# Row scales kept on chip for the gates, and the low parts of k stored on all 128 partitions for the score products

## The chip, the cores and the metric

The kernel runs on one core of a Trainium2 chip. The metric is the device time of one execution in microseconds (us). Before the change it is 1217.34 us, the median of three runs that lay between 1215.89 and 1218.22 us.

The engines are named as in the profile: PE is TensorE's matmul, PEld its weight load, DVE is VectorE, ACT is ScalarE, POOL is GpSimd and SP is SyncE, which here issues most DMAs. Each engine works through its own queue in order, and waits on semaphores.

## The reference: what is computed

One transformer-like block over a sequence of S = 1024 rows and D = 1024 columns in fp32. The parts that matter here:

```python
proj = rms_norm(x, norm1_g) @ w_in            # 1024 -> 3*512 (q, k, v) + 512 (xl) + 512 (gl)
q, k = rms_norm(q, q_norm_g), rms_norm(k, k_norm_g)      # per head, 8 heads of 64
...
for blk in range(S // 128):                    # stick-breaking attention, causal
    z = einsum('bqhd,bkhd->bhqk', q[:, q0:end], k[:, :end]) / sqrt(64)
    log_one_minus = where(mask, log_sigmoid(-z), 0)
    suffix = cumsum(log_one_minus, axis=3, reverse=True) - log_one_minus
    w = where(mask, exp(log_sigmoid(z) + suffix), 0)
    out = w @ v
...
lru = rg_lru(causal_conv(xl)) * gelu(gl)       # a gated linear recurrence
x = x + concat([attn, lru]) @ w_out
x = x + square(relu(rms_norm(x, norm2_g) @ w_up)) @ w_down
```

## The kernel before

**Precision.** A matmul operand is split into a high part (rounded to fp32r) and a low part (the remainder, also fp32r). A full product is three matmuls, low by high, high by low and high by high (`mm3`, lines 70 to 73).

**Stages.** First x is loaded, transposed and split (`hTh`, `hTl`). The norm's row scale `rstd1` is not multiplied into x; it is applied after the projection. Then come the q, k, v projection of head pair 0, the xl projection with the linear recurrence (`lru_tile`), and from about 137 us to 452 us of the span a mixed stage: attention of all four head pairs, the projections of pairs 1 to 3, and the gates. The list `ORDER` (line 27) fixes the sequence in which the program traces these pieces: `Aphc` is attention of pair p, head h, rows 256c to 256c+255, `Ipt` the projection of pair p for rows 256t and on, `Gcs` gate tile c for half s, `O` and `W` load weights, `Y` sums MLP weights by DMA. From the traced program a planner at build time, with its own simulated timeline (`schedule_with_timeline_sim=True`), lays down the order of each engine's queue, so that pieces interleave. The mixed stage is followed by the output projection (about 452 to 560 us) and the MLP (to the end).

**Projection of a head pair** (`in_proj`, lines 193 to 238; it runs 16 times, 4 pairs by 4 blocks of 256 rows). Two groups of 24 matmuls give 128 rows each of q, k and v. ACT scales the rows out of PSUM into `raw`; DVE normalizes them. Then q is laid out as `qs` so that for head 0 its 64 columns of high part come first and its 64 columns of low part second, and for head 1 the other way round; k's high part is written twice side by side (`ks`, line 222), and k's low part once (`kl`, line 223, a POOL subtraction of 128x128 for each 128 rows). PE transposes these by multiplying with the identity (lines 228, 233 and 237), and the results are copied to `qT` (ACT, line 229), `kH` (DVE, line 234, 128x512) and `kL` (DVE, line 238, 128x256). So `qT[:, h]` holds high and low part of head h on two halves of the 128 partitions, `kH[:, h]` holds the high part of k on both halves, and `kL` holds head 0's low part on partitions 0 to 63 and head 1's on 64 to 127.

**Scores** (`attention`, lines 431 to 434). For 128 query rows and up to 512 key rows a score product is two matmuls that add into one PSUM bank z: `qT[:, h]` by `kH[:, h]` over all 128 partitions, which gives (high + low of q) by high of k, and `qT[hs, h]` by `kL[hs]` over the 64 partitions of this head, which gives high of q by low of k. On the diagonal a third, bf16 matmul adds the mask (line 434). There are 96 such products. Then ACT computes two sigmoids (lines 436, 437), DVE a reversed product scan (line 441), POOL a multiplication (line 442), PE transposes the weights (line 452), ACT and DVE split them (lines 456, 457) and PE multiplies with v (line 461).

**Row scales.** `scale_row` (line 259) writes `rstd1` to DRAM as `rs_d`, from where it is read as one row broadcast to 128 partitions. In the recurrence part the tile `rsb` (128x1024) is loaded that way (line 355); it lives in the pool `lru`, which is closed before the attention. In `gate` (line 479, eight times) a 128x512 tile `y` is loaded from `rs_d` again (line 483, issued by SP); SP must first wait until the buffer, which shares the tag `raw` with `in_proj`, is free. Then DVE multiplies the projection in PSUM by it (line 487, out `gx`).

Of the kernel before, what the change touches and what calls it, by code (L numbers as in the profile page):

```python
# [9 lines left out]
F32 = mybir.dt.float32  # L10
# [9 lines left out]
P = 128  # L20
# [23 lines left out]
def kernel(ctx, tc, x, norm1_g, w_in, conv_w, conv_b, w_rg, b_rg, w_ig, b_ig,  # L44
# [106 lines left out]
    hTh = hp.tile([P, KC, S], F32R, name="hTh")  # L151
    hTl = hp.tile([P, KC, S], F32R, name="hTl")
    qkvE = pool(left1, "qkvE")
    wp = pool(left1, "wp", bufs=8)
    mp = pool(left1, "misc")

# [31 lines left out]

    def in_proj_open(p, qp):
        return (qp.tile([P, 2, S], F32R, tag="qT", name=f"qT{p}"), qp.tile([P, 2, S], F32R, tag="kH", name=f"kH{p}"),  # L190
                qp.tile([P, S], F32R, tag="kL", name=f"kL{p}"), qp.tile([P, NT, 2, P], F32R, tag="vv", name=f"vv{p}"))

    def in_proj(p, qkv, ws, tp):
        qT, kH, kL, vv = qkv
        raw = mp.tile([P, 2, 4, HD], F32, tag="raw", name=f"raw{p}{tp}", bufs=2)
        for tt in range(2):
            t = 2 * tp + tt
            pd = bank(ps_d, [384], f"pd{p}{t}")
            for kc in range(KC):
                wh, wl = ws[kc]  # L200
                mm3(pd, hTh[:, kc, t * P:(t + 1) * P], hTl[:, kc, t * P:(t + 1) * P], wh, wl, kc == 0, kc == KC - 1)
            rs = rstd1[:, t:t + 1]
            nc.scalar.mul(raw[:, tt].rearrange("p a d -> p (a d)"), pd[:, 0:256], rs)
            pvv = pd[:, 256:384].rearrange("p (h d) -> p h d", h=2)
            nc.scalar.mul(vv[:, t, :, 0:HD], pvv, rs)
            nc.vector.scalar_tensor_tensor(vv[:, t, :, HD:P], pvv, rs, vv[:, t, :, 0:HD].bitcast(F32), op0=ALU.mult, op1=ALU.subtract)  # L206
        sq = mp.tile([P, 8, HD], F32, tag="sq", name=f"sq{p}{tp}")
        raw8 = raw.rearrange("p t a d -> p (t a) d")
        nc.vector.tensor_tensor(sq, raw8, raw8, op=ALU.mult)
        ssq = small.tile([P, 8], F32, tag="ssq8", name=f"ssq{p}{tp}")  # L210
        nc.vector.tensor_reduce(ssq, sq, axis=AX.X, op=ALU.add)
        rstd = rsqrt_mean(ssq, HD, 8)
        nc.vector.tensor_tensor(raw8, raw8, rstd.unsqueeze(2).broadcast_to([P, 8, HD]), op=ALU.mult)
        nc.gpsimd.tensor_tensor(raw[:, :, 0:2, :], raw[:, :, 0:2, :], qkg, op=ALU.mult)
        qs = mp.tile([P, 2, 2, 2, HD], F32R, tag="qs", name=f"qs{p}{tp}")
        ks = mp.tile([P, 4, 2, HD], F32R, tag="ks", name=f"ks{p}{tp}")
        kl = mp.tile([P, 2, 2, HD], F32R, tag="kl", name=f"kl{p}{tp}")
        for h in range(2):
            nc.scalar.copy(qs[:, :, h, h, :], raw[:, :, h, :])
            lo_part(nc.vector, qs[:, :, h, 1 - h, :], raw[:, :, h, :], qs[:, :, h, h, :])  # L220
        for tt in range(2):
            nc.scalar.copy(ks[:, 2 * tt:2 * tt + 2], raw[:, tt, 2:4, :].unsqueeze(2).broadcast_to([P, 2, 2, HD]))
            lo_part(nc.gpsimd, kl[:, tt], raw[:, tt, 2:4, :], ks[:, 2 * tt:2 * tt + 2, 0, :])
        cols = slice(256 * tp, 256 * tp + 256)
        pq = bank(ps_t, [2, 256], f"pq{p}{tp}")
        for h in range(2):
            for tt in range(2):
                nc.tensor.matmul(pq[:, h, tt * P:(tt + 1) * P], qs[:, tt, h].rearrange("p a d -> p (a d)"), identr, start=True, stop=True)
        nc.scalar.copy(qT[:, :, cols], pq)
        pk = bank(ps_t, [2, 256], f"pk{p}{tp}")  # L230
        for h in range(2):
            for tt in range(2):
                nc.tensor.matmul(pk[:, h, tt * P:(tt + 1) * P], ks[:, 2 * tt + h].rearrange("p a d -> p (a d)"), identr, start=True, stop=True)
        nc.vector.tensor_copy(kH[:, :, cols], pk)
        pl = bank(ps_t, [256], f"pl{p}{tp}")
        for tt in range(2):
            nc.tensor.matmul(pl[:, tt * P:(tt + 1) * P], kl[:, tt].rearrange("p a d -> p (a d)"), identr, start=True, stop=True)
        nc.vector.tensor_copy(kL[:, cols], pl)


    right1 = ExitStack()
# [108 lines left out]

    lstack = ExitStack()
    lp = pool(lstack, "lru", bufs=2, side="right")
    rsb = lp.tile([P, S], F32, name="rsb", bufs=1)
    for ch in range(2):
        nc.sync.dma_start(rsb[:, 512 * ch:512 * ch + 512], rs_row[:, 512 * ch:512 * ch + 512].broadcast_to([P, 512]))
    bd = {}
# [57 lines left out]
    def attention(p, h, c, qkv):  # L414
        qT, kH, kL, vv = qkv
        hs = slice(HD * h, HD * h + HD)
        os = slice(HD - HD * h, P - HD * h)
        wrow = []
        for r in (2 * c, 2 * c + 1):
            n = (r + 1) * P  # L420
            wps = {}
            nxt = None
            qr = slice(r * P, (r + 1) * P)
            for k0 in range((n - 1) // 512 * 512, -1, -512):
                kn = min(n - k0, 512)
                diag = k0 + kn == n
                g = ap.tile([P, 516], F32, tag="g", name=f"g{p}{h}{r}{k0}", bufs=NG)
                w = ap.tile([P, 512], F32, tag="w", name=f"w{p}{h}{r}{k0}", bufs=NW)
                wps[k0 // 512] = w
                z = bank(ps_z, [512], f"z{p}{h}{r}{k0}")[:, :kn]  # L430
                nc.tensor.matmul(z, qT[:, h, qr], kH[:, h, k0:k0 + kn], start=True, stop=False)
                nc.tensor.matmul(z, qT[hs, h, qr], kL[hs, k0:k0 + kn], start=False, stop=not diag)  # L432
                if diag:
                    nc.tensor.matmul(z[:, kn - P:kn], identb, maskb, start=False, stop=True)  # L434
                    nc.gpsimd.memset(g[:, kn:kn + 1], 1.0)
                nc.scalar.activation(g[:, :kn], z, AF.Sigmoid, scale=-1.0)  # L436
                nc.scalar.activation(w[:, :kn], z, AF.Sigmoid)
                if not diag:
                    nc.vector.tensor_copy(g[:, kn:kn + 1], nxt)
                gr = g[:, :kn][:, ::-1]  # L440
                nc.vector.tensor_tensor_scan(gr, gr, gr, g[:, kn:kn + 1], op0=ALU.mult, op1=ALU.bypass)  # L441
                mark(nc.gpsimd.tensor_tensor(w[:, :kn], w[:, :kn], g[:, 1:kn + 1], op=ALU.mult))  # L442
                nxt = g[:, 0:1]
            wrow.append(wps)
        av = bank(ps_a, [256], f"av{p}{h}{c}")
        for m in range(c + 1):
            pw = bank(ps_w, [512], f"pw{p}{h}{c}{m}")

            blocks = [(0, 0), (0, 1), (1, 0), (1, 1)] if m < c else [(0, 0), (0, 1), (1, 1)]
            for i, (jj, rr) in enumerate(blocks):  # L450
                j = 2 * m + jj
                nc.tensor.transpose(pw[:, i * P:(i + 1) * P], wrow[rr][j // 4][:, j % 4 * P:(j % 4 + 1) * P], ident)  # L452
            nw = len(blocks) * P
            wth = ap.tile([P, 512], F32R, tag="wth", name=f"wth{p}{h}{c}{m}", bufs=2)
            wtl = ap.tile([P, 512], F32R, tag="wtl", name=f"wtl{p}{h}{c}{m}", bufs=2)
            nc.scalar.copy(wth[:, :nw], pw[:, :nw])  # L456
            lo_part(nc.vector, wtl[:, :nw], pw[:, :nw], wth[:, :nw])
            for jj in range(2):
                q0 = P if jj == 1 and m == c else 0
                for wt in (wtl, wth):  # L460
                    nc.tensor.matmul(av[:, q0:256], vv[:, 2 * m + jj, h, :], wt[:, 256 * jj:256 * jj + 256 - q0],  # L461
                                     start=m == 0 and jj == 0 and wt is wtl,
                                     stop=m == c and jj == 1 and wt is wth)
        ot = ap.tile([P, 256], F32, tag="ot", name=f"ot{p}{h}{c}", bufs=2)
        ob = ap.tile([P, 256], F32, tag="ob", name=f"ob{p}{h}{c}", bufs=2)
        nc.scalar.copy(ot[hs], av[os])
        nc.vector.tensor_tensor(ob[hs], av[hs], ot[hs], op=ALU.add)
        r0 = P * p + HD * h
        nc.sync.dma_start(mix_d[r0:r0 + HD, 256 * c:256 * c + 256], ob[hs])
# [9 lines left out]
    def gate(c, ch):  # L479
        s0 = 512 * ch  # L480
        y = mp.tile([P, 512], F32, tag="raw", name=f"gx{c}{ch}", bufs=2)
        hs = mp.tile([P, 512], F32, tag=("ks", "kl")[c % 2], name=f"hl{c}{ch}")
        nc.sync.dma_start(y, rs_row[:, s0:s0 + 512].broadcast_to([P, 512]))
        nc.sync.dma_start(hs, lru_d[c * P:(c + 1) * P, s0:s0 + 512])
        pd = proj_cols(gw[c // 2 * 2], c % 2, ch, f"pgl{c}{ch}")
        t = mp.tile([P, 512], F32, tag=("sq", "qs")[c % 2], name=f"ge{c}{ch}")
        nc.vector.tensor_tensor(y, pd, y, op=ALU.mult)
        nc.scalar.activation(t, y, AF.Square, scale=math.sqrt(0.044715))
        nc.vector.scalar_tensor_tensor(t, t, 1.0, y, op0=ALU.add, op1=ALU.mult)
        nc.scalar.activation(t, t, AF.Sigmoid, scale=c2)  # L490
# [384 lines left out]
```

## Time and profile before

The profiled execution took 1218.14 us; its instructions span 1216.4 us.

| engine | busy us | share of the span |
|---|---|---|
| PE | 1150.6 | 95% |
| PEld | 948.0 | 78% |
| DVE | 897.3 | 74% |
| POOL | 586.5 | 48% |
| ACT | 568.5 | 47% |

How to read the rows that follow: a group row gives line, engine, operation, out<-in with shapes and count, then busy us and mean ns of one, then the engine's idle time before them and what ended it. A row of the timeline gives start, duration, engine, line and operation. A matmul's duration contains its pipeline's depth, so that two matmuls in a row overlap: what one costs PE is the distance from its start to the start of the next. The table by stage gives busy time of each engine in a stretch of the span, the granted TensorE clock (PEclk, 1.00 is full speed) and the DMA share. The chain of waits follows the work that ended last back to the start.

### The profile page before, as it was taken

The page shows a single profiled execution, that of the slowest core. Times are in us where ns is not written, and L with a number is a line of the kernel's source. Part 1 is how long each engine was busy: PE and PEld are TensorE (multiplying, and loading weights), DVE is VectorE, ACT ScalarE, POOL GpSimd, SP SyncE. Part 2 cuts the span into 40 slices and gives each one's busy share as a digit, 9 for nine tenths or more (in the row PEclk, how much of TensorE's full clock was granted, in tenths as well). Part 3 has the DMA queues.
Part 4 walks back from the last instruction along what each step waited for, and adds up shares of the span by engine and source line. Part 5 has one row for each costly group of instructions (what it writes and reads, how often), then busy time and mean ns, then how long its engine had stood idle before and what let it go on. Part 6 is the DMA issues. An engine that isn't in the chain of part 4 may idle for free.

```text
span 1216.4 us, 15273 instructions
## 1 busy us (share of the span) xinstructions
PE 1150.6 (95%) x5410; PEld 948.0 (78%) x5410; DVE 897.3 (74%) x1182; ACT 568.5 (47%) x991; POOL 586.5 (48%) x472
## 2 busy tenths in 40 slices
PE   7998899999999988998999989889999999999998
PEld 7976777789987766886888767678887887878887
DVE  6889997999898788226387769685843876699663
ACT  7554475665665564144433554233334335733331
POOL 1356764574355566102645746533317368483240
PEclk9999999799999978998999989989999999999999
DMA  8110026824505275200453788944412345442531
GB/s 262 48 49 35 18 96 130 227 66 145 122 5 112 89 256 181 101 1 35 141 188 130 201 241 287 224 142 139 141 35 87 122 144 191 158 148 73 193 132 69
DMA packets 91659, 157.05 MB, mean 129 GB/s; under 512 B 8848, under 2 KB 27328, under 8 KB 91584
## 3 DMA queue, kind: packets, MB, share of 16 engines
q1 hardware_dynamic: 79040, 122.54, 30.5%
q0 software_dynamic: 12544, 33.56, 11.8%
q8 instruction: 42, 0.69, 0.2%
q14 instruction: 33, 0.27, 0.1%
HBM read 145.58 MB, written 44.04 MB: 156 GB/s over the span
## 4 chain that ended last, share of the span: by engine, by line
PE 69%; DVE 13%; issue 8%; DMA 3%; POOL 3%; ACT 3%; SPq 0%; DVEq 0%; ACTq 0%; POOLq 0%
PE p L633 22%; PE pa L633 11%; PE pb L633 5%; PE pc L633 4%; PE pd L71 3%; PE pd L72 3%; PE pd L73 3%; PE po L71 3%; PE po L72 2%; PE po L73 2%; PE av L461 2%; PE z L432 2%; PE pw L452 2%; DVE g L441 2%; DVE sl_u L60 2%
## 5 line engine op out<-in xcount | busy, mean ns | idle before, releaser
L442 POOL TENSOR_TENSOR w<-w,g 128x128 f32<-128x128 f32 (+3 forms) x96 | 99.7, 1044 | 107.7 <-DVE g L441 52.7
L60 DVE TENSOR_TENSOR ml_p<-rp,mh_p 128x1024 fp32r<-128x1024 f32 x56 | 110.3, 1971 | 28.1 <-ACT mh_p L544 28.1
L441 DVE TENSOR_TENSOR_SCAN g<-g 128x128 f32<-128x128 f32 (+3 forms) x96 | 112.6, 1185 | 8.0 <-ACT g L436 5.4
L544 ACT CAST sh_p<-U 128x1024 fp32r<-128x1024 f32 x48 | 50.5, 1051 | 131.0 <-PE pa L633 59.2
L633 PE MATMUL pa<-mh_p,sl_p 128*128 128x512 f32 x256 | 100.7, 393 | 7.1 <-DVE sl_p L60 6.8
L767 POOL TENSOR_TENSOR rp<-rp,qp 128x1024 f32<-128x1024 f32 x24 | 69.0, 2876 | 70.3 <-DMA qp<-in_w_down_dram 39.8
L633 PE MATMUL pa<-ml_p,sh_p 128*128 128x512 f32 x256 | 100.3, 392 | 0.0
L633 PE MATMUL pa<-mh_p,sh_p 128*128 128x512 f32 x256 | 100.1, 391 | 0.0
L71 PE MATMUL pd<-wh_p,hTl 128*128 128x384 f32 x256 | 90.9, 356 | 7.3 <-DVE vv L206 5.0
L72 PE MATMUL pd<-wl_p,hTh 128*128 128x384 f32 x256 | 89.8, 351 | 0.1
L73 PE MATMUL pd<-wh_p,hTh 128*128 128x384 f32 x256 | 88.3, 345 | 0.0
L60 DVE TENSOR_TENSOR sl_p<-U,sh_p 128x1024 fp32r<-128x1024 f32 x38 | 63.4, 1668 | 30.7 <-ACT sh_p L544 30.7
L737 POOL TENSOR_TENSOR ru<-ru,rv 128x1024 f32<-128x1024 f32 x16 | 43.8, 2769 | 58.9 <-DMA rv<-sum_u 58.8
L544 ACT CAST mh_p<-rp 128x1024 fp32r<-128x1024 f32 x56 | 58.7, 1048 | 21.3 <-POOL rp L767 14.6
L633 PEld LDWEIGHTS pa<-mh_p,sl_p 128*128 128x128 f32 x256 | 48.5, 189 | 18.2 <-DVE sl_p L60 7.5
L662 POOL TENSOR_TENSOR U<-U 128x512 f32<-128x512 f32 x32 | 47.0, 1501 | 32.0 <-ACT U L660 32.0
L456 ACT CAST wth<-pw 128x512 fp32r<-128x512 f32 (+1 forms) x80 | 42.4, 545 | 38.0 <-PE pw L452 24.8
L436 ACT ACTIVATE g<-z 128x384 f32<-128x384 f32 (+3 forms) x96 | 47.8, 497 | 22.9 <-PE z L434 10.4
L71 PEld LDWEIGHTS pd<-wh_p,hTl 128*128 128x128 f32 x256 | 49.4, 193 | 11.0 <-DVE vv L206 6.7
L660 ACT ACTIVATE U<-U 128x512 f32<-128x512 f32 x48 | 30.0, 628 | 58.6 <-DVE U L721 31.1
L60 DVE TENSOR_TENSOR wtl<-pw,wth 128x512 fp32r<-128x512 f32 (+1 forms) x80 | 49.5, 629 | 9.5 <-ACT wth L456 8.9
L633 PEld LDWEIGHTS pa<-mh_p,sh_p 128*128 128x128 f32 x256 | 48.5, 189 | 10.2
(325 smaller groups left out, 3566.7 us busy)
## 6 DMA issues: line engine op xcount, KB each, us to landing
sum_u<-in_w_up_dram POOLq DMA_DIRECT2D x8, 2048.0 KB, 12.7
sum_d<-in_w_down_dram POOLq DMA_DIRECT2D x8, 2048.0 KB, 13.3
rp<-in_w_down_dram SPq DMA_DIRECT2D x32, 512.0 KB, 4.1
rp<-sum_d SPq DMA_DIRECT2D x24, 512.0 KB, 5.4
ra<-in_w_up_dram SPq DMA_DIRECT2D x16, 512.0 KB, 4.4
qp<-in_w_down_dram SPq DMA_DIRECT2D x16, 512.0 KB, 4.2
wr_p<-in_w_in_dram SPq DMA_DIRECT2D x24, 192.0 KB, 5.8
xt<-in_x_dram SPq DMA_DIRECT2D x8, 512.0 KB, 7.5
```

The costliest lines, as they stand in the source:

```text
L60: ins = eng.tensor_tensor(lo, src, hi.bitcast(F32), op=ALU.subtract)
L71: nc.tensor.matmul(ps, al, bh, start=start, stop=False)
L72: nc.tensor.matmul(ps, ah, bl, start=False, stop=False)
L73: nc.tensor.matmul(ps, ah, bh, start=False, stop=stop)
L436: nc.scalar.activation(g[:, :kn], z, AF.Sigmoid, scale=-1.0)
L441: nc.vector.tensor_tensor_scan(gr, gr, gr, g[:, kn:kn + 1], op0=ALU.mult, op1=ALU.bypass)
L442: mark(nc.gpsimd.tensor_tensor(w[:, :kn], w[:, :kn], g[:, 1:kn + 1], op=ALU.mult))
L544: nc.scalar.copy(hl[0], src)
L633: nc.tensor.matmul(ps, x_, y_, start=start and n == 0, stop=stop and n == 2, skip_group_check=True)
L662: mark(nc.gpsimd.tensor_tensor(c, c, c, op=ALU.mult))
L737: mark(nc.gpsimd.tensor_tensor(r, r, q, **add))
L767: mark(nc.gpsimd.tensor_tensor(r, r, q, **add))
```

## The change

The tile `rsb` moves to the pool that holds `hTh`, so that it lives until the gates; `gate` multiplies by it, and its load from `rs_d` goes. `kl`, its transposes and `kL` get a second copy: each head's low part of k then lies on both halves of the 128 partitions, as its high part does, and the second matmul of a score product takes all 128 partitions. It then gives (high + low of q) by low of k, one small term more than before.

```diff
     qkvE = pool(left1, "qkvE")
+    rsb = hp.tile([P, S], F32, name="rsb")
...
-                qp.tile([P, S], F32R, tag="kL", name=f"kL{p}"), qp.tile([P, NT, 2, P], F32R, tag="vv", name=f"vv{p}"))
+                qp.tile([P, 2, S], F32R, tag="kL", name=f"kL{p}"), qp.tile([P, NT, 2, P], F32R, tag="vv", name=f"vv{p}"))
...
-        kl = mp.tile([P, 2, 2, HD], F32R, tag="kl", name=f"kl{p}{tp}")
+        kl = mp.tile([P, 4, 2, HD], F32R, tag="kl", name=f"kl{p}{tp}")
...
-            lo_part(nc.gpsimd, kl[:, tt], raw[:, tt, 2:4, :], ks[:, 2 * tt:2 * tt + 2, 0, :])
+            lo_part(nc.gpsimd, kl[:, 2 * tt:2 * tt + 2], raw[:, tt, 2:4, :].unsqueeze(2).broadcast_to([P, 2, 2, HD]),
+                    ks[:, 2 * tt:2 * tt + 2])
...
-        pl = bank(ps_t, [256], f"pl{p}{tp}")
-        for tt in range(2):
-            nc.tensor.matmul(pl[:, tt * P:(tt + 1) * P], kl[:, tt].rearrange("p a d -> p (a d)"), identr, start=True, stop=True)
-        nc.vector.tensor_copy(kL[:, cols], pl)
+        pl = bank(ps_t, [2, 256], f"pl{p}{tp}")
+        for h in range(2):
+            for tt in range(2):
+                nc.tensor.matmul(pl[:, h, tt * P:(tt + 1) * P], kl[:, 2 * tt + h].rearrange("p a d -> p (a d)"), identr, start=True, stop=True)
+        nc.vector.tensor_copy(kL[:, :, cols], pl)
...
-    rsb = lp.tile([P, S], F32, name="rsb", bufs=1)
...
-                nc.tensor.matmul(z, qT[hs, h, qr], kL[hs, k0:k0 + kn], start=False, stop=not diag)
+                nc.tensor.matmul(z, qT[:, h, qr], kL[:, h, k0:k0 + kn], start=False, stop=not diag)
...
-        nc.sync.dma_start(y, rs_row[:, s0:s0 + 512].broadcast_to([P, 512]))
...
-        nc.vector.tensor_tensor(y, pd, y, op=ALU.mult)
+        nc.vector.tensor_tensor(y, pd, rsb[:, s0:s0 + 512], op=ALU.mult)
```

## The prediction

> **What bounds the kernel now.** I read the page's chain of waits first, then the table by stage around the score products, then the chain inside those stages.
>
> ```profile
> PE 69%; DVE 13%; issue 8%; DMA 3%; POOL 3%; ACT 3%; SPq 0%; DVEq 0%; ACTq 0%; POOLq 0%
> ```
>
> ```profile
> 20.00:137.00 117.00, 111.39 (x549) 93.29 (x548) 105.78 (x217) 69.43 (x138) 59.24 (x69) 1.00 0.20 60
> 137.00:200.00 63.00, 56.55 (x299) 45.83 (x297) 58.83 (x113) 32.92 (x83) 36.67 (x52) 0.97 0.37 100
> 200.00:230.00 30.00, 27.25 (x147) 21.59 (x147) 26.80 (x41) 19.15 (x46) 14.99 (x22) 0.94 0.60 162
> 230.00:362.00 132.00, 132.00 (x754) 113.48 (x753) 119.47 (x231) 80.99 (x197) 69.46 (x97) 0.94 0.40 102
> 362.00:400.00 38.00, 36.28 (x201) 30.02 (x199) 31.24 (x66) 21.07 (x57) 22.00 (x36) 0.96 0.43 90
> 400.00:452.00 52.00, 45.64 (x227) 34.18 (x227) 44.27 (x58) 31.31 (x67) 34.24 (x36) 0.91 0.58 201
> ```
>
> The columns are stretch, length, then busy PE, PEld, DVE, ACT, POOL, clock and DMA. From 230 to 362 us PE is never idle. DVE is busy 119.5 of 132 us there, so PE binds with DVE 12.5 us behind it. From 137 to 200 us DVE is the fuller one (58.8 of 63), and after 362 us neither is full. Over 137 to 452 us DVE sums to 280.6 of 315 us: 34.4 us idle. The chain agrees, first for 230 to 362 us, then for 137 to 450 us:
>
> ```profile
> by line: PE pd L73 15.8%; PE pd L71 15.7%; PE pd L72 15.5%; PE av L461 13.3%; PE z L432 12.9%; PE pw L452 11.3%; PE z L431 7.7%; PE z L434 3.5%; PE pq L228 1.8%; PE pk L233 1.6%; PE pl L237 0.7%; DVE sq L209 0.5%
> ```
>
> ```profile
> by line: issue 9.7%; PE av L461 7.6%; PE z L432 7.3%; PE pd L73 7.1%; PE pd L71 7.1%; PE pd L72 7.0%; DVE g L441 6.5%; PE pw L452 5.9%; PE z L431 4.5%; DMA gx<-rs_d 3.7%; DVE wtl L60 2.2%; PE z L434 1.9%; PE pgl L71 1.8%; PE pgl L72 1.8%; P
> ```
>
> In the first, everything but 0.5% is PE. Score products (L431, L432, L434) hold 24.1% of it, 31.8 us; in the second 13.7% of 313 us, 42.9 us. So only 11.1 us of chain time in score products lie outside 230 to 362 us. The MLP, the longest part, is untouched.
>
> **Part 1, the score products: what a 64-row matmul costs.** Here is a product of 512 keys and then one gate projection:
>
> ```profile
> 380.61 0.44 PE L432 MATMUL z<-kL,qT 64*128 64x384 f32 x1
> 380.98 0.23 PE L434 MATMUL z<-maskb,identb 128*128 128x128 bf16 x1
> 381.02 0.48 PE L431 MATMUL z<-kH,qT 128*128 128x512 f32 x1
> 381.43 0.49 PE L432 MATMUL z<-kL,qT 64*128 64x512 f32 x1
> 381.85 0.23 PE L434 MATMUL z<-maskb,identb 128*128 128x128 bf16 x1
> 381.89 0.48 PE L71 MATMUL pgl<-hTh,wl_gl 128*128 128x512 f32 x1
> 382.21 0.40 PE L72 MATMUL pgl<-hTl,wh_gl 128*128 128x512 f32 x1
> 382.44 0.39 PE L73 MATMUL pgl<-hTh,wh_gl 128*128 128x512 f32 x1
> ```
>
> ```profile
> 381.43 0.18 PEld L432 LDWEIGHTS z<-kL,qT 64*128 64x128 f32 x1 [0.24 <-issue]
> 381.86 0.20 PEld L71 LDWEIGHTS pgl<-hTh,wl_gl 128*128 128x128 f32 x1
> 381.98 0.19 PEld L72 LDWEIGHTS pgl<-hTl,wh_gl 128*128 128x128 f32 x1
> ```
>
> ```profile
> 225.78 0.31 PE L431 MATMUL z<-kH,qT 128*128 128x128 f32 x1
> 226.02 0.33 PE L432 MATMUL z<-kL,qT 64*128 64x128 f32 x1
> 226.27 0.23 PE L434 MATMUL z<-maskb,identb 128*128 128x128 bf16 x1
> ...
> 406.43 0.64 PE L233 MATMUL pk<-identr,ks 128*128 128x128 f32 x4
> 406.90 0.45 PE L73 MATMUL pgl<-hTh,wh_gl 128*128 128x512 f32 x1
> ```
>
> ```profile
> L432 PE MATMUL z<-kL,qT x96: 322/491/793, 137.4 to 445.9; 64*128 64x512 f32 x48, 64*128 64x128 f32 x16, 64*128 64x256 f32 x16, 64*128 64x384 f32 x16
> ```
>
> Whole-array matmuls of 512 columns that add into one bank follow each other at 0.23 us (382.21 to 382.44). L431 to L432 takes 0.41 and L432 to L434 takes 0.42: 0.18 and 0.19 lost, 0.37 a product. The weight load shows why: L432's is not begun before its own matmul's start, after 0.24 us of nothing, while L72's load at 381.98 runs under the matmul of 381.89. The step from 128 rows to 64 rows and the step back both empty the array. The step L434 to L71, bf16 to fp32r, costs 0.04, so it is the rows and not the type. For 384 keys one side takes 0.37 against three quarters of 0.23, 0.17: 0.40 for two sides. For 128 keys it is 0.24 and 0.25 against 0.12 (four L233 from 406.43 to 406.90): 0.25. For 256 I take the middle, 0.33. In all 48 x 0.37 + 16 x 0.40 + 16 x 0.33 + 16 x 0.25 = 33.4 us of PE time that whole-array products do not need.
>
> **What of it reaches the end.**
>
> ```profile
> 230.00:362.00 132.00, 19.88 (x41) 8.26 (x41) 0.94 0.40 102
> ```
>
> This row counts L432 alone: 41 of 96 products lie where PE binds, 14.3 us. DVE is next late. It has 12.5 us of idle time there, less what the change adds to it (1.3 us by its copies and up to 2.8 us by POOL, both below), so 8.4 to 11.2 us. As the queues are in order, DVE will not fill every gap: I take 7, bounds 0 and 11. Outside, a product's stall is 0.37 of its 0.83 us, 45%, so of the 11.1 us in the chain 5 are stall; I take 4, bounds 0 and 5. The other stalls lie beside DVE's work and buy nothing.
>
> **Part 2, the second copy of k's low part.**
>
> ```profile
> L237 PE MATMUL pl<-identr,kl x32: 222/275/327, 47.9 to 411.9; 128*128 128x128 f32 x32
> ...
> L238 DVE CAST kL<-pl x16: 387/410/426, 48.3 to 413.3; 128x256 fp32r<-128x256 f32 x16
> ...
> L234 DVE CAST kH<-pk x16: 628/674/691, 43.9 to 407.1; 128x512 fp32r<-128x512 f32 x16
> ```
>
> ```profile
> L60 POOL TENSOR_TENSOR kl<-raw,ks 128x128 fp32r<-128x128 f32 x32 | 17.4, 565 | 7.8 <-PE pl L237 6.4 <-ACT wth L456 1.1 <-ACT w L437 0.3
> ...
> L214 POOL TENSOR_TENSOR raw<-raw,qkg 128x256 f32<-128x256 f32 x16 | 11.8, 739 | 41.6 <-DVE raw L213 13.4 <-DVE rs_m L96 13.4 <-DVE rs_m L95 13.1
> ```
>
> ```profile
> 230.00:362.00 132.00, 2.02 (x5) 0.94 0.40 102
> ```
>
> PE gets 32 more transposes at 0.12 us, 3.8 us in all. DVE's copy grows from L238's 410 to L234's 674 ns: 16 x 0.264 = 4.2 us. POOL's subtraction grows from 565 ns to about L214's 739 (twice as long at the most): 32 x 0.17 to 0.28, 5.6 to 8.8 us. The last row counts L238 between 230 and 362 us: five projections, 1.2 us of PE, 1.3 us of DVE and 1.7 to 2.8 us of POOL. PE's 1.2 us comes off the 14.3, which leaves 13.1, still more than DVE's slack. Behind a later `kl`, PE's L237 waits, and behind it the products of the queue; L237's waits today name other engines, and one POOL step is only some 0.2 us longer. Outside this stretch lie 11 projections; at 0.26 + 0.24 + 0.34 us each, 9 us if nothing covered them. PE or DVE work covers most; I charge 2.5, bounds 0 and 9.
>
> **Part 3, the row scales.**
>
> ```profile
> DVE gx L487 <- DMA gx<-rs_d: 4.5, 3, 3.3
> ```
>
> ```profile
> 192.44 7.48 DMA gx<-rs_d
> ...
> 411.79 4.11 DMA gx<-rs_d
> ```
>
> ```profile
> SPq L483 <- POOL kl L60: 18.6, 3, 9.8
> ```
>
> Eight loads go, with SP's waits for their buffer, which hold back what SP issues behind them. DVE loses 4.5 us to them in three waits, the longest 3.3. The chain passes through two of the loads, 11.6 us, but DVE had other work under most of that, so the waits are the ceiling: I take 3, bounds 0 and 4.5. After them the projection's own matmuls and DVE's turn are next late. `rsb` is loaded as before, by the same two DMAs at the same place; its own memory adds no wait.
>
> **Sum.** 7 + 4 + 3 - 2.5 = 11.5 us off the profiled execution's 1218.1 us. That one lies 0.8 us above the median, so from the median, 1217.3, I forecast 1206 us.
>
> **Rivals.** (a) All of PE's time passes on: DVE's gaps shrink with PE, since they follow PE's results. Then 13 us inside, 5 outside and 4.5 for the loads come, and DVE's early stretch gives 4 more: 26 us, 1191 us. For it: 34 us of DVE idle in 315. Against it: DVE at 93% from 137 to 200 us and 91% from 230 to 362.
>
> (b) DVE takes over at once. Gaps that are only latency (scan, POOL, transpose, split) stay; 2 us in all remain: 1215 us. For it: the same 91%.
>
> (c) The stall stays, so the change does not do what it says. The Trainium skill, TensorE: Matmul & The Clock Gate, Part 3 (The mechanism), says that weight loads overlap running matmuls only when the row groups differ; by that rule a whole-array load would wait just as L432's does today. The result would be 3 us won, 2.5 lost: 1217 us. Against it stands the load at 381.98, which ran under a whole-array matmul. By that row the trace contradicts the page here.
>
> (d) Slower, by POOL and DVE excluding each other:
>
> ```profile
> 186.56 1.27 DVE L441 TENSOR_TENSOR_SCAN g<-g 128x512 f32<-128x512 f32 x1
> 188.13 2.02 DVE L441 TENSOR_TENSOR_SCAN g<-g 128x512 f32<-128x512 f32 x1
> ...
> 187.98 1.09 POOL L442 TENSOR_TENSOR w<-w,g 128x512 f32<-128x512 f32 x1 [2.24 <-DVE g L441]
> ```
>
> The scan of 188.13 took 0.75 us longer than its like, about until POOL's operation ended at 189.07. If every longer `kl` holds up a scan, DVE pays 4.2 + 5.6 to 8.8 us; where DVE's gaps are latency, all of it shows and PE's saving does not: 1218 + 10, less up to 3 for the loads, 1225 us. It decides once DVE, not PE, is the last to finish from 230 us on. For it: the 91%. Against it: PE's unbroken 132 us. The Trainium skill's page SBUF — State Buffer, SBUF: two separate sides, calls the shared port pair an exclusive lock for the whole instruction; the two scans agree with that.
>
> **Numbers.** The forecast gets 0.62, (a) 0.13, (b) 0.12, (c) 0.04, (d) 0.09. A measurement of this kernel tells about 0.2% from no change, 2.4 us. Half of (b) falls on each side of that line: faster 0.80, same 0.11, slower 0.09. The forecast's own terms run from 11 + 5 + 4.5 = 20 us won to some 3 lost; with (a) in and (d) out the range is 1190 to 1217 us. The planner may order queues anew, and the granted clock (0.91 to 0.97 in these stages) may shift with PE's gaps; both are inside the range.
>
> **What would show it.** In the profile after: L431 to L432 and L432 to its successor at 0.23 us for 512 columns, L432's load before its matmul; no wait of L487 on a DMA; `kl` at about 0.74 us, L238 at 0.67; PE no longer without a gap in what was 230 to 362 us, and DVE above 95% there. The stage that ends at 452 us should end near 440. I am wrong if L432's distance stays at 0.4, if PE still binds after saving 30 us (then (a)), or if DVE's scans get longer (then (d)).

## The result, and the profile after

The changed kernel takes **1225.46 us** (median of 17 runs, 1220.12 to 1230.26), the kernel before 1218.08 (17 runs): ratio 1.0071, 95% interval 1.0056 to 1.0087. It is slower by about 0.7%, where I had forecast 1% faster. Ratios here and below leave out the few executions far off the rest (1379.96 to 3580.32 us), medians do not. The profiled execution after took 1222.91 us, its span is 1221.1; the clock granted over the span is nearly that of before (0.972, before 0.969).

The page's chain of waits after:

```profile
PE 63%; DVE 18%; issue 7%; DMA 5%; ACT 3%; POOL 3%; SPq 0%; DVEq 0%; POOLq 0%; ACTq 0%
```

PE's share fell from 69 to 63%, DVE's rose from 13 to 18%. The table by stage, in the same stretches and columns as before:

```profile
20.00:137.00 117.00, 103.17 (x501) 86.33 (x499) 99.16 (x205) 61.81 (x125) 57.25 (x66) 0.95 0.20 59
137.00:200.00 63.00, 57.05 (x296) 49.29 (x296) 61.56 (x114) 32.58 (x78) 37.34 (x46) 0.92 0.22 74
230.00:362.00 132.00, 120.26 (x753) 110.02 (x752) 121.11 (x231) 77.50 (x194) 72.10 (x93) 0.96 0.43 109
```

PE is now idle for 12 of the 132 us from 230 on, and DVE, at 121.1, is not full either (92%; I had said above 95%). The first row shows a loss that I had not looked for: in the front (what runs ahead of the mixed stage), PE does 103.2 us of work instead of 111.4 and DVE 99.2 instead of 105.8. The first score product tells how late the front ends, first before, then after:

```profile
137.25 0.22 PE L431 MATMUL z<-kH,qT 128*128 128x128 f32 x1
```

```profile
151.03 0.22 PE L433 MATMUL z<-kH,qT 128*128 128x128 f32 x1
151.09 0.27 PE L434 MATMUL z<-kL,qT 128*128 128x128 f32 x1
```

It is 13.8 us late. The last product of the attention (`av`) ends only 2.9 us late, at 463.9 instead of 461.0 us: the mixed stage wins back 11 us.

The stall itself went, as far as it came from the rows. PE's timeline after, a product behind a mask matmul and one behind a projection, then the weight loads of the second:

```profile
343.98 0.23 PE L436 MATMUL z<-maskb,identb 128*128 128x128 bf16 x1
344.02 0.48 PE L433 MATMUL z<-kH,qT 128*128 128x512 f32 x1
344.33 0.40 PE L434 MATMUL z<-kL,qT 128*128 128x512 f32 x1
344.56 0.34 PE L73 MATMUL pd<-wh_p,hTh 128*128 128x384 f32 x1
...
348.89 0.39 PE L433 MATMUL z<-kH,qT 128*128 128x512 f32 x1
349.12 0.39 PE L434 MATMUL z<-kL,qT 128*128 128x512 f32 x1
349.35 0.33 PE L72 MATMUL pd<-wl_p,hTh 128*128 128x384 f32 x1
```

```profile
343.98 0.20 PEld L433 LDWEIGHTS z<-kH,qT 128*128 128x128 f32 x1
344.10 0.19 PEld L434 LDWEIGHTS z<-kL,qT 128*128 128x128 f32 x1
...
348.72 0.19 PEld L433 LDWEIGHTS z<-kH,qT 128*128 128x128 f32 x1
348.90 0.19 PEld L434 LDWEIGHTS z<-kL,qT 128*128 128x128 f32 x1
```

The second step (L434 to its successor) takes 0.23 at both places, and L434's load (348.90) runs under the matmul before it. The first step is 0.23 behind a projection, but 0.31 behind a mask: there L433's own load begins only with the mask's matmul, at 343.98. The kernel before had shown the same: L71, behind the mask of 381.85, takes 0.32 to L72 (381.89 to 382.21).

Why the front is late shows first on SP's queue, before and after:

```profile
27.82 15.84 SPq L259 DMA_DIRECT2D rs_d<-rstd  x2
51.26 0.34 SPq L163 DMA_DIRECT2D wr_xl<-in_w_in_dram  x1
51.70 2.59 SPq L355 DMA_DIRECT2D rsb<-rs_d  x2
54.38 1.33 SPq L163 DMA_DIRECT2D wr_xl<-in_w_in_dram  x3
```

```profile
35.32 0.34 SPq L357 DMA_DIRECT2D rsb<-rs_d  x1
41.67 0.36 SPq L262 DMA_DIRECT2D rs_d<-rstd  x1
52.99 0.33 SPq L357 DMA_DIRECT2D rsb<-rs_d  x1
53.41 1.81 SPq L164 DMA_DIRECT2D wr_xl<-in_w_in_dram  x4
```

```profile
SPq L357 <- DMA rs_d<-rstd: 18.9, 2, 10.9
```

Before, one of four weight loads went ahead of the two `rsb` loads and three stood behind them. After, the planner put the `rsb` loads ahead of all four. It did so in each traced build that it planned freely with the tile in the pool of `hTh` (the first `rsb` load goes at 36.37 us in `e1_rows` and at 35.31 in `best_free`, both below), and not in `e2_klow`, where the tile stays in the recurrence's pool (52.66). That memory which is free earlier is the reason is likely, but not shown. The second `rsb` load waits 10.9 us for the store of 41.67 to land, and the first of the weights behind it goes at 53.41 instead of 51.26; the last of the four goes no later than before. ACT's split of that first weight, before, then ACT's wait after between 48 and 70 us and DVE's between 50 and 70:

```profile
55.21 0.41 ACT L164 CAST wh_xl<-wr_xl 128x256 fp32r<-128x256 f32 x1 [3.67 <-DMA wr_xl<-in_w_in_dram]
```

```profile
ACT wh_xl L165 <- DMA wr_xl<-in_w_in_dram: 7.4, 1, 7.4
```

```profile
DVE sq L210 <- ACT raw L204: 4.4, 1, 4.4
```

ACT's split of those weights stands ahead of pair 0's `raw`, for which DVE then waits 4.4 us. Before, the same split started 2.3 us earlier (55.21, after 57.52), and DVE's waits in this stretch name no `raw`.

### The profile page after: what moved, and what is told of

Its sections match the earlier page's. It is cut to its first block, busy times and chain, and to the rows that moved or that the text cites. A ratio compares the mean times of both kernels' runs of the same rounds, so it can differ in the third digit from the quotient of the medians.

```text
span 1221.1 us, 15310 instructions
## 1 busy us (share of the span) xinstructions
PE 1124.9 (92%) x5442; PEld 942.7 (77%) x5442; DVE 907.5 (74%) x1182; ACT 564.4 (46%) x991; POOL 594.8 (49%) x472
## 4 chain that ended last, share of the span: by engine, by line
PE 63%; DVE 18%; issue 7%; DMA 5%; ACT 3%; POOL 3%; SPq 0%; DVEq 0%; POOLq 0%; ACTq 0%
PE p L634 21%; PE pa L634 11%; PE pb L634 4%; PE pc L634 4%; DVE g L443 3%; PE po L71 3%; PE po L73 2%; PE po L72 2%; PE pd L72 2%; PE pd L73 2%; PE pd L71 2%; DMA wr_p<-in_w_in_dram 2%; PE av L463 2%; PE pw L454 2%; DVE sl_u L60 1%
## 5 line engine op out<-in xcount | busy, mean ns | idle before, releaser
L444 POOL TENSOR_TENSOR w<-w,g 128x128 f32<-128x128 f32 (+3 forms) x96 | 104.8, 1104 | 77.9 <-DVE g L443 40.1
L443 DVE TENSOR_TENSOR_SCAN g<-g 128x128 f32<-128x128 f32 (+3 forms) x96 | 112.6, 1186 | 5.6 <-ACT g L438 2.8
L71 PE MATMUL pd<-wh_p,hTl 128*128 128x384 f32 x256 | 90.8, 357 | 8.8 <-DVE vv L207 4.3
L72 PE MATMUL pd<-wl_p,hTh 128*128 128x384 f32 x256 | 91.5, 357 | 0.0
L71 PEld LDWEIGHTS pd<-wh_p,hTl 128*128 128x128 f32 x256 | 49.8, 195 | 13.1 <-DVE vv L207 5.6
L454 PE MATMUL pw<-ident,w 128*128 128x128 f32 x288 | 47.7, 285 | 10.2 <-DVE wtl L60 7.8
```

The costliest lines, as they stand in the source:

```text
L71: nc.tensor.matmul(ps, al, bh, start=start, stop=False)
L72: nc.tensor.matmul(ps, ah, bl, start=False, stop=False)
```

## The experiments

I had three theories. **Work**: what the change adds costs more than it wins. **Stall**: the whole-array products win nothing. **Order**: the work wins, and the planner, which lays every queue anew for the changed program, gives it back. Ratios are to the kernel before, run on the same chip; 0.1% is 1.2 us.

**The parts alone, planned freely.** `e1_rows` has only the moved `rsb` and the gates that read it; `e2_klow` only the second copy and the whole-array products. `e3_copy64` is the kernel after with

```diff
-                nc.tensor.matmul(z, qT[:, h, qr], kL[:, h, k0:k0 + kn], start=False, stop=not diag)
+                nc.tensor.matmul(z, qT[hs, h, qr], kL[hs, h, k0:k0 + kn], start=False, stop=not diag)
```

and `e5_whole_nocopy` the kernel before with whole-array products against the one copy of k's low part (the other head's rows meet the low part of q, a term far below the result's accuracy):

```diff
-                nc.tensor.matmul(z, qT[hs, h, qr], kL[hs, k0:k0 + kn], start=False, stop=not diag)
+                nc.tensor.matmul(z, qT[:, h, qr], kL[:, k0:k0 + kn], start=False, stop=not diag)
```

> Only the row scales: rsb lives with hTh and the gates multiply by it, no second copy of k's low part, 64-row products. The first score product came 14 us later in the changed kernel, and the recurrence before it, too. Theory A1 (the loss comes with rsb: its load is now issued ahead of the xl weights and SP waits on rs_d before it can issue them, and the planner lays the front out anew): first score product at 145 to 152 us, 1222 to 1230 us. Rival A2 (the loss is the second copy's work in the projections): first score product at 137 us as before, 1213 to 1217 us by the loads that are gone.

> Only the second copy of k's low part and the whole-array products; rsb stays in the recurrence's pool and the gates load their rows. Theory A1: front as before but for some 2 us, the products' saving shows: 1207 to 1213 us. Rival A2: the front is late as in the changed kernel, first score product at 145 to 152 us, 1222 to 1230 us.

> The changed kernel with its queues in exactly the same order, but the second score matmul again on the 64 partitions of its head (the copy is made and half of it is read). Theory A: the stalls come back and what the whole-array product won in this order is lost, 1232 to 1240 us against 1225 of the changed kernel. Rival B: 1224 to 1227 us.

> The kernel before with one line changed: the second score matmul takes all 128 partitions of qT[:, h] against kL as it is stored (head 0's low part on one half, head 1's on the other). Nothing is copied, nothing moved, and every queue keeps its order. The product gains a term, the low part of q of one head by the low part of k of the other, about as small as the terms that are left out anyway. Theory A (the 64-row matmul empties the array, and PE binds between 230 and 362 us): 7 us inside that stretch and up to 5 outside, 1204 to 1211 us. Rival B (DVE binds or every gap is latency, so PE's saving buys nothing): 1216 to 1219 us. In both, L431 to L432 falls from 0.41 to 0.23 us.

Measured: `e1_rows` 1221.57 us (1.0038, 1.0019 to 1.0056), `e2_klow` 1228.59 (1.0098, 1.0075 to 1.0121), `e3_copy64` 1229.61 (1.0102, 1.0081 to 1.0124), `e5_whole_nocopy` 1213.68 (0.9971, 0.9952 to 0.9990). `e3_copy64` has the queue orders of the kernel after, `e5_whole_nocopy` those of the kernel before: whole-array products win 0.3%, some 4 us, in either order, so the theory Stall is out. Both runs lie between their two theories: the products win something, but less than A gave. `e1_rows` comes out just under A1's time, with its first score product at 142.6 us; `e2_klow` falls to A2 (145.3 us), although its `rsb` stays in the old pool, so a late front needs no moved load. But the row scales, which only take work away, cost 4.6 us, and the two halves' prices (4.6 and 11.9) don't add up to the whole's 8.6. That speaks for Order, but does not show it.

**The same work in the other kernel's order.** For every engine the instructions of one kernel were taken in the order in which another kernel issues them, and each was tied to the one before it by an edge that orders issue alone and adds no wait between engines:

```python
for p, i in zip(queue, queue[1:]):
    tc.add_manual_dep(i, p.name, mybir.DependencyInfo(mybir.DependencyClass.NoSync, mybir.DependencyReason.DATA), reason="queue order")
```

`a_in_b`: the kernel after's work in the kernel before's orders (added transposes behind their sisters). `b_in_a`: the reverse. `rows_in_b` and `klow_in_b`: the work of `e1_rows` and of `e2_klow` in the kernel before's orders.

> All of the change's work (row scales kept, second copy, whole-array products), but with every engine's queue laid by added issue-order edges as in the kernel before; the 32 added transposes stand behind their sisters. Theory A (the loss is the planner's new order, the work itself gains): the products alone gave 1213.7 us in this order, the copy costs about 2.5, the row scales give 0 to 3: 1209 to 1217 us, first score product at 137 to 140 us. Theory B (the loss is the added work): 1221 to 1228 us as in the kernel after.

> The kernel before's work, with every engine's queue laid as in the kernel after; only its eight loads of row scales, which the kernel after has not, find their own place on SP. Theory A (order): slower than before by 7 to 14 us, 1224 to 1231 us, first score product near 150 us. Theory B (work): within 3 us of before, 1215 to 1220 us.

> Row scales kept on chip alone (64-row products, one copy of k's low part), queues laid as in the kernel before; planned freely this work took 1221.6 us. Theory A (order): 1213 to 1218 us. Theory B (the moved tile or the gates' reading of it costs by itself): 1220 to 1223 us.

> Second copy and whole-array products alone (row scales loaded as before), queues laid as in the kernel before; planned freely this work took 1228.6 us. Theory A (order): 1213.7 plus 0 to 5 for the copy, 1213 to 1219 us. Theory B (the longer copies on POOL, PE and DVE cost it): 1224 to 1230 us.

Measured: `a_in_b` 1213.84 us (0.9970, 0.9951 to 0.9988), `b_in_a` 1251.96 (1.0303, 1.0279 to 1.0326), `rows_in_b` 1214.29 (0.9980, 0.9963 to 0.9997), `klow_in_b` 1220.16 (1.0035, 1.0016 to 1.0054). The same work is 12 us faster in before's order (1.0071 to 0.9970), and its first score product starts at 139.4 us instead of 151.0. The row scales alone now win 2.4 us instead of losing 4.6. Order is the larger cause. The parts say the same: the planner's own order costs the row scales 0.58% (1.0038 to 0.9980, 7.1 us) and the second copy with its products, whose `rsb` did not move, 0.63% (1.0098 to 1.0035, 7.7 us). `b_in_a`, slower than both theories said, shows more than order: its `rsb` still lies in the recurrence's pool, and its eight gate loads found places of their own, for which DVE waits 31.4 us (4.5 in the kernel before). `klow_in_b` fell between the theories: the copy costs 0.64% against `e5_whole_nocopy`, some 8 us, more than Order allowed.

**Where in the order.** In `front_in_b` only the instructions ahead of the first attention step (some 260 places change) stand as before, in `rest_in_b` only those behind it; `rsb_late` is the kernel after with the two `rsb` loads behind the weights on SP, the other four queues unchanged.

> The kernel after with its own queues, except that the instructions of the front (all that stands in the code before the first attention step: norm, pair 0, recurrence) take their places in the order that they have in the kernel before; some 260 of 8,509 instructions change place. All of after's work in before's queues throughout took 1213.8 us, the kernel after 1225.5. Theory A (the loss lies in the front's order): first score product near 139 us instead of 151, 1212 to 1218 us. Rival (the order counts as much in the mixed stage): first score product near 139 us too, but 1218 to 1224 us.

> The mirror of the run before: the kernel after with its own order in the front, and the instructions behind the front in the order of the kernel before. Theory A (front): first score product stays near 151 us, 1222 to 1228 us. Rival (order of the mixed stage): first score product near 151 us, but 1214 to 1220 us.

> The kernel after with its own queues on TensorE, VectorE, ScalarE and GpSimd, and on SyncE the two loads of the row scales moved behind the eight first weight loads of the recurrence, so that no weight load stands behind their wait for the row scales' store (18.9 us in the kernel after). Theory A1 (the head-of-line wait on SyncE's queue is what makes the front late): first score product near 140 us, 1213 to 1218 us. Theory A2 (the front is late by the order on VectorE, ScalarE and TensorE): first score product 147 to 151 us, 1221 to 1227 us.

Measured: `front_in_b` 1220.16 us (1.0028, 1.0013 to 1.0043), `rest_in_b` 1224.18 (1.0075, 1.0046 to 1.0104), `rsb_late` 1219.04 (1.0027, 1.0011 to 1.0043). The first score product starts at 140.0, 146.4 and 145.7 us. SP's queue in `rsb_late`:

```profile
27.69 15.16 SPq L262 DMA_DIRECT2D rs_d<-rstd  x2
50.21 3.97 SPq L164 DMA_DIRECT2D wr_xl<-in_w_in_dram  x4
54.28 0.86 SPq L357 DMA_DIRECT2D rsb<-rs_d  x2
```

ACT's split of the first weight behind the old wait then starts at 54.68 instead of 57.52, and DVE's wait for `raw` falls from 4.4 to 0.3 us:

```profile
54.68 0.41 ACT L165 CAST wh_xl<-wr_xl 128x256 fp32r<-128x256 f32 x1 [3.74 <-DMA wr_xl<-in_w_in_dram]
```

Two loads moved on one queue give back 0.44%, 5 us, as much as the whole front in before's order. Neither A1 nor A2 fits whole: the head-of-line wait (a queue works in order, so what stands behind a waiting load waits too) is nearly half of the 12 us. `front_in_b` falls to the rival (order counts in the mixed stage too), `rest_in_b` by its time to theory A (alone it gives nothing), although its first score product comes 4.6 us earlier than the expected 151: the other 7 us (`rsb_late` 1.0027 against `a_in_b` 0.9970) come back only with both stretches in before's order. Which places in them matter stays open.

**Without the second copy.** `best_in_b` joins `rows_in_b` and `e5_whole_nocopy`: the whole diff against the kernel before is that of `e5_whole_nocopy`, `rsb` in the pool of `hTh`, and the gates' two lines. `best_again` is the same kernel beside other runs. `best_free` is its work with no edge, `best_late` ties the two `rsb` loads behind `loads[0]`, the last of the eight weight loads:

```diff
+        if c == 0:
+            with tc.issue_after(loads[0]):
+                for ch in range(2):
+                    nc.sync.dma_start(rsb[:, 512 * ch:512 * ch + 512], rs_row[:, 512 * ch:512 * ch + 512].broadcast_to([P, 512]))
```

> Row scales kept on chip and whole-array products against the single copy of k's low part (each product then also adds the low part of q times the other head's low part of k, a term far below the result's accuracy), queues as in the kernel before. Alone the two gave 1214.3 and 1213.7 us in this order, against 1216.8 to 1217.7. Theory A (the gains add): 1209 to 1212 us. Rival (both gains fill the same slack of VectorE): 1212.5 to 1215 us.

> The kernel of best_in_b once more, beside the run that follows, as that run's base on the same chip: 1205 to 1209 us if its first six runs were typical; 1209 to 1212 if they were on the fast side, and then most of the copy's price of 6 us is smaller too.

> The work of best_in_b with no edge added, the planner free. Theory A (the planner gives back what the change wins, since the early row-scale loads stand ahead of weight loads on SyncE and every queue behind is laid anew): 1213 to 1221 us. Rival (the planner's order hurts only together with the second copy): 1206 to 1210 us.

> The work of best_in_b with one pair of edges: the two loads of the row scales are issued behind the last of the recurrence's eight first weight loads; the other four queues are the same as in best_free. Theory A1 (the head-of-line wait on SyncE): 4 to 7 us faster than best_free. Theory A2 (order elsewhere): within 2 us of best_free.

Measured: `best_in_b` 1206.82 us (0.9918, 0.9891 to 0.9945), `best_again` 1207.14 (0.9923, 0.9898 to 0.9947), `best_free` 1216.92 (1.0004, 0.9989 to 1.0020), `best_late` 1211.67 (0.9956, 0.9938 to 0.9973). This version beats both kernels, by more than either theory had expected. The gains do not fill the same slack: 0.20% and 0.29% alone, 0.8% together; what goes beyond their sum, 0.3%, is no larger than its uncertainty. Left to itself the planner gives all of it back, without any second copy, and although the first score product starts at 139.7 us, nearly as early as in `best_again` (138.8), so a late start of the attention is not the only way in which order costs; the two edges, with the other four queues laid exactly as in `best_free`, keep 0.48% of it. The stages of `best_again`, from 230 us on:

```profile
230.00:362.00 132.00, 121.72 (x782) 113.11 (x781) 121.52 (x237) 80.39 (x200) 72.39 (x99) 0.99 0.38 95
```

PE has 782 matmuls there instead of 754 and is idle 10 us, DVE too: neither is full. The chain of waits of this stretch names DVE's scan (18.6%), the DMA that stores the attention's results, `mix_d` (17.4%), and issue (14.6%) first.

**What of the copy costs.** All against `best_in_b`, in its order. `pool_in_b` makes GpSimd's subtraction 256 elements wide and leaves the second half unused; `pool4_in_b` 512 elements, three quarters unused; `pedve_in_b` adds the 32 transposes and DVE's wider copy, GpSimd staying at 128 elements:

```diff
-        kl = mp.tile([P, 2, 2, HD], F32R, tag="kl", name=f"kl{p}{tp}")
+        kl = mp.tile([P, 4, 2, 2, HD], F32R, tag="kl", name=f"kl{p}{tp}")
...
-            lo_part(nc.gpsimd, kl[:, tt], raw[:, tt, 2:4, :], ks[:, 2 * tt:2 * tt + 2, 0, :])
+            lo_part(nc.gpsimd, kl[:, :, tt], raw[:, tt, 2:4, :].unsqueeze(1).broadcast_to([P, 4, 2, HD]),
+                    ks[:, 2 * tt:2 * tt + 2, 0, :].unsqueeze(1).broadcast_to([P, 4, 2, HD]))
...
-                nc.tensor.matmul(pl[:, tt * P:(tt + 1) * P], kl[:, tt].rearrange("p a d -> p (a d)"), identr, start=True, stop=True)
+                nc.tensor.matmul(pl[:, tt * P:(tt + 1) * P], kl[:, 0, tt].rearrange("p a d -> p (a d)"), identr, start=True, stop=True)
```

> best_in_b with GpSimd's subtraction for kl written twice as wide (256 elements, as in the change) and its second half unused: what the change adds on GpSimd alone. Queues as before, best_in_b took 1206.8 us (0.992 of before), the whole copy with everything else 1213.8 (0.997). Theory P (GpSimd's longer subtraction, which VectorE's operations exclude and are excluded by, is most of the copy's 6 to 7 us): 1210 to 1214 us. Theory D (VectorE's and TensorE's share is): 1206 to 1208.5 us.

> best_in_b with the change's 32 further transposes and its copy of 512 columns for kL, but with GpSimd's subtraction at 128 elements: what the change adds on TensorE and VectorE alone (both copies then hold the two heads' rows, and each product again adds the low part of q times the other head's low part of k). Theory D: 1210 to 1214 us. Theory P: 1206 to 1209 us; VectorE's 16 x 0.264 us and TensorE's 32 x 0.12 us would be hidden in the gaps.

> best_in_b with GpSimd's subtraction for kl written four times as wide (512 elements), three quarters of it unused: the suspected cost, tripled against pool_in_b, whose 256 elements took 0.40 us longer each and measured 4.7 us. Theory P (GpSimd's time is what costs): some 1.1 us longer each, three times 4.7 us, 1217 to 1223 us. Theory D (pool_in_b's 4.7 us were chance, GpSimd's time is hidden): 1206 to 1211 us.

Measured: `pool_in_b` 1211.50 us (0.9958, 0.9943 to 0.9973), `pedve_in_b` 1209.40 (0.9939, 0.9915 to 0.9963), `pool4_in_b` 1223.34 (1.0059, 1.0037 to 1.0081). Against the mean of the two bases, 0.9920, GpSimd's double width costs 0.38% (4.6 us), the transposes and DVE's copy 0.19% (2.3 us, within the uncertainty), fourfold width 1.39% (16.9 us), just above what theory P gave. The group rows (busy us, mean ns) of GpSimd's subtraction and of a DVE operation that often falls beside it, first in `best_again`, then in `pool4_in_b`:

```profile
L60 POOL TENSOR_TENSOR kl<-raw,ks 128x128 fp32r<-128x128 f32 x32 | 15.8, 515 | 6.2 <-PE pl L238 6.1
...
L60 DVE TENSOR_TENSOR qs<-raw,qs 128x128 fp32r<-128x128 f32 x32 | 12.2, 415 | 1.7 <-ACT qs L220 1.7
```

```profile
L60 POOL TENSOR_TENSOR kl<-raw,ks 128x512 fp32r<-128x512 f32 x32 | 47.1, 1491 | 6.8 <-PE pl L239 6.6
...
L60 DVE TENSOR_TENSOR qs<-raw,qs 128x128 fp32r<-128x128 f32 x32 | 17.1, 566 | 2.1 <-ACT qs L220 2.1
```

DVE's `qs` has the same work in both and takes 4.9 us more. One place of `pool4_in_b`, DVE, then GpSimd, which is in its second subtraction until 299.02:

```profile
298.30 1.07 DVE L60 TENSOR_TENSOR qs<-raw,qs 128x128 fp32r<-128x128 f32 x2
```

```profile
296.48 2.54 POOL L60 TENSOR_TENSOR kl<-raw,ks 128x512 fp32r<-128x512 f32 x2
```

In `best_again` such a pair of `qs` takes 0.48 us:

```profile
289.13 0.48 DVE L60 TENSOR_TENSOR qs<-raw,qs 128x128 fp32r<-128x128 f32 x2
```

Pairing every DVE instruction of the first 470 us with itself in the two traces (the queues are the same, 778 pairs), their durations grew by 20.4 us in sum (the scans by 5.3), the 634 of ACT by -1.7, for 31.2 us more on GpSimd's `kl`. Between `best_in_b` and `best_again`, the same kernel, the sum over DVE differs by 0.8 us. So two thirds of GpSimd's added time return as longer DVE instructions beside it: theory P. How much of the 16.9 us comes by that way, and how much by work that waits for GpSimd itself, no run separates.

## Why the prediction was wrong, point by point

**The step that failed** is the last one on the range, that the planner's new order is inside it: I priced the work and gave the order no term. It is the largest: 1.0071 - 0.9970 is 12.3 us. With it failed the sentence "`rsb` is loaded as before, by the same two DMAs at the same place; its own memory adds no wait". The first of the two loads went from 51.70 to 35.32 us, the second to 52.99, both now ahead of all four weight loads. Undoing that alone gives back 5 of the 12 us (`rsb_late`); where in the order the other 7 lie stays open.

The range did not follow from its own bounds either. With every gain at 0 and the copy at its bound of 9 the sum loses 9 us, not "some 3", which reaches 1226 us; and 3 us lost would have been 1220, not 1217. (The chances add to 0.81 faster and 0.10 same, not 0.80 and 0.11.)

**The sum, re-made from the runs:** products and row scales in before's order -9.7 us (0.9920), the second copy +6.1 (0.9920 to 0.9970), the order +12.3 (0.9970 to 1.0071): 8.7 us. That these three add up to the measured 0.71% is by construction; what the runs add is the sizes, and these depend on which of the three steps is taken first. My terms were -14, +2.5 and nothing.

- *Part 1, the stall.* Right that the rows cause it and that it goes; 33.4 us was a little much. By the medians of the step in the two traces (48 products of 512, 16 of each shorter size) both steps together took 69.4 us before and 40.8 after: 28.6. The 0.41 of the first step was not all rows: 0.31 stays behind a mask, whose switch I had set at 0.04, though 0.32 stood in my own rows (381.89 to 382.21).
- *What reaches the end.* I added 7, 4 and 3 as if independent. Alone they measured 3.5 (products) and 2.4 us (row scales), together 9.7, of my 14. The 3.8 us beyond the sum are no larger than their uncertainty, so whether each gain needs the other stays open.
- *Part 2, the copy.* The mis-sized term is GpSimd's. I took 739 ns for a `kl`; the median is 740, but the mean in the kernel after is 888 against 565 before, so it is 32 x 0.32 = 10 us more and not 5.6 to 8.8 (12 in `pool_in_b` against `best_again`). And "PE or DVE work covers most" is wrong for it: DVE is what it holds up. In before's order the term measured 4.6 us, the transposes and the DVE copy together 2.3; the sum of 6.1 to 6.9 lay inside my bounds of 0 and 9, far from the 2.5.
- *Part 3, the row scales.* Forecast 3, measured 2.4 in before's order, and lost 4.6 in the planner's own.
- *The signs I had named.* Load ahead of the matmul, `kl` at 0.74 (median), the copy at 0.67, no wait of a gate for its row scales: seen. Steps at 0.23: seen for the second, for the first only where no mask stands ahead. DVE above 95% and the stage's end near 440: not seen. For the front, where a part of the time went, I had named no sign.

**The rivals.** (a) did not come: PE gets 28.6 us, of which 3.5 reach the end alone and about 7 beside the row scales (9.7 less their 2.4). (b) holds in part: 10 us of both engines stay idle from 230 to 362 even in `best_again`. (c) is out. The Trainium skill's rule for it, TensorE: Matmul & The Clock Gate, Part 3 (The mechanism), would have a whole-array load wait for the matmul in flight; L434's load at 348.90 does not, as the load at 381.98 of the kernel before had not. The same section also names a load into the background weight buffer as one that goes ahead of running matmuls; read with that, these rows agree with it. (d) gave 1225 us, the number that was measured, but it is not its cause: its mechanism is real, as `pool4_in_b` shows, and in before's order worth 4.6 us; the 12 of the order it does not have. The sign I had named for it, longer scans, did not come: their mean is 1185 ns before and 1186 after. The Trainium skill, SBUF — State Buffer, SBUF: two separate sides, says that within the engine side only the port pair that DVE shares with GpSimd causes contention; DVE's +20.4 and ACT's -1.7 us agree with it.

That `best_in_b` takes my 1206 us is luck: it lacks the copy, for which my sum had charged 2.5. The whole work in the order of before, which is what my sum described, takes 1213.84 (`a_in_b`): a smaller gain and a dearer copy than I had added up, and still inside my range.

## What to carry to other kernels

Where a planner lays the queues, a change has a third cost beside its work and its waits: the order that comes out. Ask of every tile that changes its pool when its loads may now be issued, and what they will stand ahead of; and before judging an edit, measure its work in the old order, by edges that fix issue alone. Work put on GpSimd beside a busy DVE was not hidden here: it cost the kernel 4.6 us for 12 us more of it, 16.9 for 31.

## What the hardware showed that I had not expected

- The same instructions in two issue orders differ by 12 us of 1218 (`a_in_b` against the kernel after), and moving two loads of one queue is worth 5 to 6 us of it, twice over (`rsb_late`, and `best_late` against `best_free`).
- Behind a bf16 matmul the next fp32r load starts only with that matmul (343.98; over the 64 masks of the kernel after, a median of 2 ns behind its start), which costs the following step 0.08 us (0.31 against 0.23).
- `kl`'s mean on GpSimd at 256 elements is 888 ns in the kernel after and 894 in `pool_in_b`, beside a median of 740: each of the ten that took over 850 ns in the kernel after (up to 1658) lies beside a scan or another DVE instruction that reads SBUF twice or copies, so a median hides what the neighbour costs.
